# A decoder trunk on one core: where ScalarE's lead copies and two of its table loads stand in the queue

## The chip, the cores and the metric

The kernel runs on one core of one Trainium2 chip. The core's engines work beside each other, each on its own list of instructions in order, and wait for one another through semaphores: TensorE (PE in the profile, its weight loads PEld), VectorE (DVE), ScalarE (ACT), GpSimd (POOL) and SyncE (SP), which here issues most of the transfers from memory. The metric is the device time of one execution in microseconds (us). The time before is the median of three runs.

## What is computed

The reference is a decoder trunk of two layers for 512 tokens of width 1024 in float32. Every layer is a mixer between two half-step SwiGLU feed-forward networks (FFNs) of inner width 2816, each behind an RMSNorm; the mixer of the first layer is a gated linear attention (GLA), that of the second a stick-breaking attention (SB).

```python
def swiglu(h, w_gate, w_up, w_down):
    return (jax.nn.silu(h @ w_gate) * (h @ w_up)) @ w_down
...
    for i in range(DEPTH):
        x = x + 0.5 * swiglu(rmsnorm(x, ffn1_norm[i]), ffn1_w_gate[i], ffn1_w_up[i], ffn1_w_down[i])
        h = rmsnorm(x, mix_norm[i])
        ...
        x = x + y.astype(x.dtype)
        x = x + 0.5 * swiglu(rmsnorm(x, ffn2_norm[i]), ffn2_w_gate[i], ffn2_w_up[i], ffn2_w_down[i])
    return rmsnorm(x, final_norm)
```

## The kernel before

**Numbers in two parts.** Every float32 operand of a large product is split into a high part in the format fp32r, which ScalarE makes by a cast, and a low part, the difference, which VectorE makes by a subtraction. A product is then three matmuls: high by high, low by high, high by low (`mm3`, and `prod` in the blocks below).

**Weights.** `Feed` holds a queue of entries. An entry is a piece of a weight matrix with the products that use it. `Feed.start` (from line 139) takes the next entry, and for it and the entries just behind it has the raw weights loaded into tile `raw` or `rawd` by SyncE (line 91), and cut into the tiles `wh` and `wl`, of which there are four each (`Entry.split`: the cast is line 126, the subtraction line 127). So casts run ahead of the products, as far as buffers allow: a cast has to wait until PE no longer needs the `wh` that it overwrites.

**The FFN blocks.** Most of the gate and up products are made in `FFN.seven` (products in line 692): a block of 256 columns by 512 tokens is made from seven half-size products in place of eight, on sums and differences of weights (DVE, lines 675 to 682, tile `s`) and of activations. A block is two entries. `body_1` starts with the product on tile `ps_w`, which ScalarE copies to `ps_z` (line 716) before PE goes on adding to both, then one on `ps_q` (line 719), again `ps_w` (line 722) and `ps_z`. `body_2` adds a third time to `ps_w`, ScalarE copies that state to `u3` (line 734, u in the profile), PE makes the 12 matmuls of the last product on `ps_q`, and then adds to `ps_w` once more. That last product overwrites what line 734 reads, so PE has to wait until the copy is done. `gate` (line 702) applies Silu on ScalarE, or multiplies with the gate on VectorE (line 705). The down products are made in `down` (line 66, tile `ps_d`) and in `seven_down` (line 367), which is built like `seven` with its copies in lines 385 and 409.

**The lead copy.** The first matmul of a block that follows a product of another kind takes its weights not from `wh` but from a small tile of its own, `first` (128 by 128, tag `w1`, one buffer): it holds the same numbers as the first 128 columns of that entry's first `wh`, made from `raw` by a second ScalarE copy (line 132). The profile calls this copy w<-raw, 32 of them in the run.

**Activations.** `FFN.cut` (line 785) splits activations: the cast on ScalarE is line 786, the subtraction on VectorE line 787. `close`, `close_first` and `close_second` use it for the products of an FFN, `normed_input` and `sums` for its input.

**Tables.** ScalarE needs a table of functions loaded for Silu, another for Exp and Ln, another for Sqrt. Two loads are written out by hand and ordered behind the last Silu of an FFN: `exp_ln_tables(st["silu"])` (line 888, the load itself in line 580) at the start of an FFN that follows an FFN, which happens once, and the load of the Sqrt table in line 909, in the last FFN ahead of the last down product.

**What sets the order.** The program is traced in Python, and a planner then orders each engine's instructions by their dependences, by when it expects operands and buffers to be ready, and by the order of tracing. An instruction that it takes to be ready early moves ahead of others. `tc.issue_after(i)` gives what is traced inside it, on the engine of instruction `i`, a place behind `i` in that engine's order. It sets the order of issue only; it adds no wait for `i` to finish. Before the change the lead copy has no such mark: it depends on the raw weights and on the free tile `w1` alone, while the cast in line 126 also needs a free `wh`.

Of the kernel before, what the change touches and what calls it, by code (L numbers as in the profile page):

```python
# [18 lines left out]
P = 128  # L19
# [13 lines left out]
def decoder(ctx: ExitStack, tc: tile.TileContext, a: dict, out: bass.AP):  # L33
    nc = tc.nc
# [59 lines left out]
    class Entry:  # L94
# [14 lines left out]
        def split(self):  # L109
            if self.W is None:  # L110
                self.W = []
                for r, (_, _, n, m) in zip(self.view(), self.units):
                    few = n * m < 1024
                    if few:

                        h = st["few"].tile([P, n * m + NEAR], F32R, tag="vh", bufs=1, name="wh")[:, NEAR:]
                        l = st["few"].tile([P, n * m + 64 - NEAR], F32R, tag="vl", bufs=1, name="wl")[:, : n * m]
                    else:
                        h, l = (
                            wp.tile([P, n * m + 64], F32R, tag="w" + t, bufs=4, name="w" + t)[  # L120
                                :, self.place : self.place + n * m
                            ]
                            for t in "hl"
                        )
                    h, l = (t.rearrange("p (n m) -> p n m", m=m) for t in (h, l))
                    st["cut"] = nc.scalar.copy(h, r).ins  # L126
                    nc.vector.tensor_tensor(out=l, in0=r, in1=h.bitcast(F32), op=ALU.subtract)  # L127
                    self.W.append((h, l))
                    if self.lead and len(self.W) == 1:

                        first = wp.tile([P, P], F32R, tag="w1", bufs=1, name="w1")
                        nc.scalar.copy(first, r[:, 0, 0:P])
                        self.first = first

    class Feed:
# [321 lines left out]
    st = {}  # L457
# [79 lines left out]
    def sums_wide(pool):  # L537

        ss = st["ss"]
        h = sp.tile([P, T], F32R, tag="sq", name="sh")  # L540
        nc.scalar.copy(h, ss)
        l = pool.tile([P, T], F32R, tag="t", name="sl")
        nc.vector.tensor_tensor(out=l, in0=ss, in1=h.bitcast(F32), op=ALU.subtract)
        st["wide"] = ps = psum("ps_R")
        mm(ps, ones_r, h, True, False)
        mm(ps, ones_r, l, False, True)

    def rstd_wide():

        ps = st["wide"]  # L550
        v = sp.tile([P, T], F32, tag="ss", name="v")
        nc.vector.tensor_scalar(out=v, in0=ps, scalar1=1.0 / D, scalar2=EPS, op0=ALU.mult, op1=ALU.add)
        y = st["R"] = sp.tile([P, T], F32, tag="sq", name="R")
        act(y, v, AF.Ln)
        act(y, y, AF.Exp, scale=-0.5)
        nc.scalar.activation(ps, y, AF.Square)
        nc.vector.scalar_tensor_tensor(out=v, in0=ps, scalar=-0.5, in1=v, op0=ALU.mult, op1=ALU.mult)
        nc.vector.scalar_tensor_tensor(out=y, in0=v, scalar=1.5, in1=y, op0=ALU.add, op1=ALU.mult)

    def two_halves(between=None):  # L560

        feed.finish()
        g = [feed.start(), feed.start()]
        for i in range(3):
            for x in g:
                next(x, None)
            if i == 0 and between is not None:
                between()

    def new_norm():  # L570
        st["h"], st["l"] = st["nh"], st["nl"]

    def flush(deferred):
        for evac, ps in deferred:
            evac(ps)
        deferred.clear()

    def exp_ln_tables(after):
        with tc.issue_after(after):
            st["tab"] = nc.scalar.preload_act_table_set("natural_log_exp_and_others").ins  # L580
# [7 lines left out]
    class FFN:  # L588
# [194 lines left out]
            return t  # L783

        def cut(self, h, l, t):
            nc.scalar.copy(h, t)
            nc.vector.tensor_tensor(out=l, in0=t, in1=h.bitcast(F32), op=ALU.subtract)
            return h, l

# [90 lines left out]
        def run(self, between=None):  # L880
            with tc.tile_pool(name="hp", bufs=8, reuse_waits="tile") as self.hp, tc.tile_pool(
                name="tp", bufs=5, reuse_waits="tile"
            ) as self.tp:
                st["few"] = self.hp
                new_norm()
                if st["ss"] is not None:
                    if self.after_ffn:
                        exp_ln_tables(st["silu"])
                    two_halves(lambda: sums_wide(self.tp))
                    rstd_wide()  # L890
                flush(self.defer)
                def spread(todo, n):
                    for i in range(n):
                        for piece in todo[i * len(todo) // n : (i + 1) * len(todo) // n]:
                            piece()
                        feed.entries(1)

                spread(self.normed_input(), self.NORMED - 2)
                self.normed = True
                st["h"], st["l"] = zip(*self.n)  # L900
                todo = self.sums()
                spread(todo[:5], self.sums_by - self.NORMED)
                feed.entries(1, True)
                for piece in todo[5:]:
                    piece()
                feed.entries(self.count - self.sums_by - 1, True)
                if between is not None:
                    with tc.issue_after(st["silu"]):
                        nc.scalar.preload_act_table_set("sqrt_and_others")
                    feed.q[feed.pos].split()  # L910
                    between(self.tp)
                feed.entries(self.total - self.count)
# [579 lines left out]
    def begin(ip):  # L1492
# [116 lines left out]
        g, u = psum("ps_f"), psum("ps_f")  # L1609
        scale(0)()  # L1610
        cut(eg, 0)()
        square(0, 1, True), square(1, 1, False)
        scale(1)(), scale(2)()
# [15 lines left out]
        pin(nc.vector.tensor_scalar(out=v, in0=v, scalar1=1.0 / D, scalar2=EPS, op0=ALU.mult, op1=ALU.add))  # L1629
        low()  # L1630
        low = cut(eu, 0)
        st["sqrt"] = pin(nc.scalar.activation(y, v, AF.Sqrt)).ins
        keep(0), keep(1), keep(2)
# [26 lines left out]
        for i in range(NT):  # L1660
# [5 lines left out]
            )  # L1666
        scale(4)()
        cut(eg, 1)()
        scale(5)(), scale(6)(), scale(7)()
        st["R"] = sp.tile([P, T], F32, tag="sq", name="R")  # L1670
# [65 lines left out]
```

## Time and profile before

| | |
|---|---|
| median of 3 runs | 1842.72 us (1842.33 to 1846.41) |
| profiled execution, its own time | 1843.01 us |
| its span, first to last instruction | 1841.2 us |
| granted TensorE clock | 0.999 |
| busy: PE, PEld, DVE, ACT | 1821.4, 1656.5, 1531.1, 1068.6 us |
| matmuls on PE | 12476 |
| instructions on ACT | 1842 |
| lead copies, line 132 | 32, mean 294 ns |
| table loads on ACT, all lines | 11, 1283 ns each |

A row of a timeline gives the start in us from the start of the span, the duration in us, the engine, the line, the operation, what it writes <- what it reads, the shapes, and in square brackets how long the engine sat idle ahead of it and what released it. A row of the waits gives who waited, for whom, the idle time in total, how many times, and the longest. In the view of one line the numbers behind an operation are its count and its shortest, median and longest duration in ns; below stands for whom its engine was idle before it, with total us and times, and who waited for it. An arrow points to the releaser. The ends of matmuls are modelled, so that their starts tell more of PE's pace than their durations.

### The profile page before, as it was taken

The page shows a single profiled execution, that of the slowest core. Times are in us where ns is not written, and L with a number is a line of the kernel's source. Part 1 is how long each engine was busy: PE and PEld are TensorE (multiplying, and loading weights), DVE is VectorE, ACT ScalarE, POOL GpSimd, SP SyncE. Part 2 cuts the span into 40 slices and gives each one's busy share as a digit, 9 for nine tenths or more (in the row PEclk, how much of TensorE's full clock was granted, in tenths as well). Part 3 has the DMA queues.
Part 4 walks back from the last instruction along what each step waited for, and adds up shares of the span by engine and source line. Part 5 has one row for each costly group of instructions (what it writes and reads, how often), then busy time and mean ns, then how long its engine had stood idle before and what let it go on. Part 6 is the DMA issues. An engine that isn't in the chain of part 4 may idle for free.

```text
span 1841.2 us, 30773 instructions
## 1 busy us (share of the span) xinstructions
PE 1821.4 (99%) x12476; PEld 1656.5 (90%) x12476; DVE 1531.1 (83%) x2509; ACT 1068.6 (58%) x1842; POOL 8.7 (0%) x20
## 2 busy tenths in 40 slices
PE   8999999999999999999999999999999999999998
PEld 7999999889888899999889999998888788999997
DVE  8999797776777989889798988976878779898885
ACT  6556555444555566555555555645878755565554
POOL 0000000100000000000000000000000000000000
PEclk9999999999999999999999999999999999999999
DMA  5333324221223233333233232322221222333331
GB/s 161 118 122 116 103 93 135 83 69 47 69 69 115 92 101 107 120 100 115 89 106 113 91 118 92 119 87 83 69 70 58 69 92 92 115 106 113 104 104 69
DMA packets 177649, 179.20 MB, mean 97 GB/s; under 512 B 4130, under 2 KB 168020, under 8 KB 177508
## 3 DMA queue, kind: packets, MB, share of 16 engines
q1 hardware_dynamic: 176800, 176.18, 30.3%
q8 instruction: 97, 1.59, 0.4%
q0 software_dynamic: 608, 1.05, 0.2%
q14 instruction: 44, 0.36, 0.1%
q10 hardware_dynamic: 100, 0.03, 0.0%
HBM read 175.17 MB, written 2.10 MB: 96 GB/s over the span
## 4 chain that ended last, share of the span: by engine, by line
PE 80%; DVE 12%; DMA 6%; ACT 2%; issue 1%; SPq 0%; DVEq 0%; ACTq 0%
PE ps_w L692 16%; PE ps_f L66 15%; PE ps_d L66 14%; PE ps_q L692 7%; PE ps_t L66 5%; DVE wl L127 4%; PE ps_z L692 4%; PE ps_b L66 4%; PE ps_w L367 3%; DMA raw<-in_ffn_w_gate_dram 3%; DMA raw<-in_ffn_w_up_dram 3%; PE ps_q L367 2%; PE ps_S L66 1%; PE ps_z L1315 1%; PE ps_bt L66 1%
## 5 line engine op out<-in xcount | busy, mean ns | idle before, releaser
L127 DVE TENSOR_TENSOR wl<-raw,wh 128x1024 fp32r<-128x1024 f32 x242 | 255.5, 1059 | 88.9 <-ACT wh L126 46.6
L126 ACT CAST wh<-raw 128x1024 fp32r<-128x1024 f32 (+1 forms) x242 | 223.0, 922 | 163.0 <-PE ps_d L66 36.5
L127 DVE TENSOR_TENSOR wl<-s,wh 128x1024 fp32r<-128x1024 f32 x176 | 213.9, 1217 | 43.4 <-PE ps_z L692 40.1
L692 PE MATMUL ps_w<-th,wh 128*128 128x256 f32 x864 | 240.1, 278 | 5.6 <-ACT u L734 5.3
L692 PE MATMUL ps_w<-tl,wh 128*128 128x256 f32 x864 | 238.8, 276 | 0.0
L692 PE MATMUL ps_w<-th,wl 128*128 128x256 f32 x864 | 238.7, 276 | 0.0
L126 ACT CAST wh<-s 128x1024 fp32r<-128x1024 f32 x176 | 184.8, 1050 | 84.0 <-DVE s L682 27.7
L66 PE MATMUL ps_f<-xh,wh 128*128 128x512 f32 x432 | 172.6, 400 | 0.0
L66 PE MATMUL ps_f<-xl,wh 128*128 128x512 f32 x432 | 169.4, 392 | 0.0
L692 PEld LDWEIGHTS ps_w<-th,wh 128*128 128x128 f32 x864 | 162.2, 188 | 8.0 <-ACT u L734 7.0
L66 PE MATMUL ps_f<-xh,wl 128*128 128x512 f32 x432 | 168.9, 391 | 0.0
L692 PEld LDWEIGHTS ps_w<-tl,wh 128*128 128x128 f32 x864 | 162.3, 188 | 0.0
L66 PE MATMUL ps_d<-hh,wl 128*128 128x512 f32 x416 | 162.2, 390 | 0.0
L692 PEld LDWEIGHTS ps_w<-th,wl 128*128 128x128 f32 x864 | 162.2, 188 | 0.0
L66 PE MATMUL ps_d<-hh,wh 128*128 128x512 f32 x416 | 162.2, 390 | 0.0
L66 PE MATMUL ps_d<-hl,wh 128*128 128x512 f32 x416 | 161.8, 389 | 0.0
L126 ACT CAST wh<-rawd 128x1024 fp32r<-128x1024 f32 (+1 forms) x84 | 81.5, 970 | 89.9 <-PE ps_d L66 48.8
L127 DVE TENSOR_TENSOR wl<-rawd,wh 128x1024 fp32r<-128x1024 f32 (+1 forms) x84 | 93.1, 1116 | 21.1 <-PE ps_z L692 12.0
L322 DVE SCALAR_TENSOR_TENSOR x<-ps_d,x 128x512 f32<-128x512 f32 x120 | 80.7, 683 | 22.1 <-PE ps_d L66 21.7
L66 PEld LDWEIGHTS ps_f<-xl,wh 128*128 128x128 f32 x432 | 81.1, 188 | 17.3
L66 PEld LDWEIGHTS ps_f<-xh,wl 128*128 128x128 f32 x432 | 81.3, 188 | 15.6
L66 PEld LDWEIGHTS ps_f<-xh,wh 128*128 128x128 f32 x432 | 81.3, 188 | 15.4
(348 smaller groups left out, 5271.4 us busy)
## 6 DMA issues: line engine op xcount, KB each, us to landing
raw<-in_ffn_w_gate_dram SPq DMA_DIRECT2D x43, 1024.0 KB, 5.4
raw<-in_ffn_w_up_dram SPq DMA_DIRECT2D x43, 1024.0 KB, 5.6
rawd<-in_ffn_w_down_dram SPq DMA_DIRECT2D x84, 512.0 KB, 3.7
raw<-in_gla_w_in_dram SPq DMA_DIRECT2D x12, 1024.0 KB, 5.3
raw<-in_sb_w_in_dram SPq DMA_DIRECT2D x16, 512.0 KB, 3.8
raw<-in_gla_w_out_dram SPq DMA_DIRECT2D x4, 1024.0 KB, 5.0
raw<-in_sb_w_in_dram SPq DMA_DIRECT2D x4, 1024.0 KB, 5.3
raw<-in_sb_w_out_dram SPq DMA_DIRECT2D x4, 1024.0 KB, 5.0
```

The costliest lines, as they stand in the source:

```text
L66: st["pe"] = nc.tensor.matmul(ps, l, r, start=first, stop=last).ins
L126: st["cut"] = nc.scalar.copy(h, r).ins
L127: nc.vector.tensor_tensor(out=l, in0=r, in1=h.bitcast(F32), op=ALU.subtract)
L322: nc.vector.scalar_tensor_tensor(out=xs[k], in0=ps, scalar=0.5, in1=xs[k], op0=ALU.mult, op1=ALU.add)
L367: st["pe"] = nc.tensor.matmul(ps, l_, r_, start=first and c + n == 0, stop=c == 1 and n == 2, skip_group_check=True).ins
L692: st["pe"] = nc.tensor.matmul(o, l_, r_, start=first and j + n == 0, stop=j == 3 and n == 2, skip_group_check=True).ins
L1315: nc.tensor.matmul(o_, l_, r_, start=first, stop=last, skip_group_check=True)
```

## The change

Three edits, all on ScalarE's order, none on what is computed. The lead copy is marked to be issued behind `st["cut"]`, which at that point is the cast (line 126) of the same raw block. `FFN.cut` keeps its latest cast as `st["closed"]`. The two hand-written table loads are marked behind that cast in place of the last Silu.

```diff
@@ Entry.split
                     if self.lead and len(self.W) == 1:
 
                         first = wp.tile([P, P], F32R, tag="w1", bufs=1, name="w1")
-                        nc.scalar.copy(first, r[:, 0, 0:P])
+                        with tc.issue_after(st["cut"]):
+                            nc.scalar.copy(first, r[:, 0, 0:P])
                         self.first = first
@@ FFN.cut
-            nc.scalar.copy(h, t)
+            st["closed"] = nc.scalar.copy(h, t).ins
             nc.vector.tensor_tensor(out=l, in0=t, in1=h.bitcast(F32), op=ALU.subtract)
@@ FFN.run
                     if self.after_ffn:
-                        exp_ln_tables(st["silu"])
+                        exp_ln_tables(st["closed"])
@@ FFN.run
                 if between is not None:
-                    with tc.issue_after(st["silu"]):
+                    with tc.issue_after(st["closed"]):
                         nc.scalar.preload_act_table_set("sqrt_and_others")
```

## The prediction, made before the changed kernel ran

> **What bounds the kernel now.** I read the page first, then the waits of PE, then the source view of the copies that the change moves, then the timelines of ACT and PE around them.
>
> ```profile
> span 1841.2 us, 30773 instructions
> PE 1821.4 (99%) x12476; PEld 1656.5 (90%) x12476; DVE 1531.1 (83%) x2509; ACT 1068.6 (58%) x1842; POOL 8.7 (0%) x20
> PE 80%; DVE 12%; DMA 6%; ACT 2%; issue 1%; SPq 0%; DVEq 0%; ACTq 0%
> ```
>
> PE sets the time from end to end. An edit on ACT, busy for 58%, is therefore worth exactly the time in which PE stands still because of ACT. PE's own waits, longest first:
>
> ```profile
> PE ps_w L692 <- ACT u L734: 5.3, 9, 1.2
> ...
> PE ps_w L367 <- ACT ps_z L385: 1.3, 2, 0.9
> ...
> PE ps_w L692 <- ACT ps_z L716: 0.4, 2, 0.2
> ```
>
> The largest wait is nine times for the copy u of line 734; two are for the copy of line 716. Neither copy is slow; what matters is what ACT was doing just before. Line 132 is the lead copy:
>
> ```profile
> L132 ACT CAST w<-raw x32: 287/293/300, 50.6 to 1757.0; 128x128 fp32r<-128x128 f32 x32
>   DMA raw<-in_ffn_w_up_dram: 11.4, 8
>   DMA raw<-in_ffn_w_gate_dram: 4.8, 5
> ```
>
> At 13 of its 32 places ACT sits idle ahead of the lead copy, 16.2 us in all, until a weight transfer lands. ACT works in order, so whatever stands behind waits too. ACT around the first such place, and the ninth of the places where PE waits:
>
> ```profile
> 86.57 0.30 ACT L132 CAST w<-raw 128x128 fp32r<-128x128 f32 x1 [1.20 <-DMA raw<-in_ffn_w_up_dram]
> 86.78 0.36 ACT L734 COPY u<-ps_w 128x256 f32<-128x256 f32 x1
> ...
> 93.56 1.05 ACT L126 CAST wh<-raw 128x1024 fp32r<-128x1024 f32 x1
> ...
> 1649.52 0.30 ACT L132 CAST w<-raw 128x128 fp32r<-128x128 f32 x1 [1.39 <-DMA raw<-in_ffn_w_up_dram]
> 1649.72 0.37 ACT L734 COPY u<-ps_w 128x256 f32<-128x256 f32 x1
> ```
>
> The lead copy waits to 86.57, u starts 0.21 us later, and the cast that reads the same raw block comes only at 93.56. So it is in the timeline at all nine PE waits for u: the instruction ahead of u is a lead copy held by its transfer. The remaining four held copies (13 less 9) cost PE nothing.
>
> **What one such stall costs.** The idle time in brackets is not the whole loss, because ends of matmuls are modelled: a product of 256 columns is shown 0.28 us long while the next starts 0.11 us after it. So I take starts:
>
> ```profile
> 86.61 0.28 PE L692 MATMUL ps_q<-nh,wl 128*128 128x256 f32 x1
> 86.72 0.28 PE L692 MATMUL ps_q<-nl,wh 128*128 128x256 f32 x1
> 87.19 0.38 PE L692 MATMUL ps_w<-th,wh 128*128 128x256 f32 x1 [0.20 <-ACT u L734]
> 87.42 0.29 PE L692 MATMUL ps_w<-th,wl 128*128 128x256 f32 x1
> 87.54 0.28 PE L692 MATMUL ps_w<-tl,wh 128*128 128x256 f32 x1
> ```
>
> From 86.72 to 87.54 are 0.82 us for three steps that take 3 x 0.113 = 0.34 elsewhere in the same stream: 0.48 lost, where 0.20 is shown. Each stall thus costs its shown idle time plus 0.28: 0.17 hidden under the modelled end (0.28 less 0.11) and 0.11 because the first product after the wait takes two steps.
>
> [...]
>
> ```profile
>   PEld ps_w L692: 7.0, 9
> ```
>
> Among those who waited for line 734, the weight loads stand with 7.0 us in nine waits: they were held along with the matmul, so I keep the 0.11.
>
> **Part 1, the lead copies.** Nothing is added or removed: 32 copies of 0.29 us (0.21 from start to start, 86.57 to 86.78) go behind a cast of the same raw block. No wait for completion is added: only their place in ACT's order changes. No DMA goes with them. On SP the next load into raw waits for the last reader of it, and behind that cast DVE still reads the block for 1.2 us in line 127, so a lead copy 0.3 us behind the cast is never last.
>
> *Removed:* nine stalls, 5.3 + 9 x 0.28 = 7.8 us. What is late next there? Without the copy in the way u starts when its product is complete, as it does at undisturbed places (rows at 110.66 and 111.82 below): it ends at 111.03, and PE, which has 12 products of ps_q to do meanwhile, overwrites the tile at 111.82. 0.79 us remain, so PE runs through.
>
> *Added:* the copy must now be ready for PE's first product. I compare cast and first use in the first and last of 32 blocks:
>
> ```profile
> 54.10 1.05 ACT L126 CAST wh<-raw 128x1024 fp32r<-128x1024 f32 x1
> ...
> 1773.02 1.05 ACT L126 CAST wh<-raw 128x1024 fp32r<-128x1024 f32 x1 [1.88 <-PE ps_w L367]
> 1774.33 1.05 ACT L126 CAST wh<-s 128x1024 fp32r<-128x1024 f32 x1 [0.26 <-PE ps_z L367]
> ```
> ```profile
> 69.16 0.28 PE L692 MATMUL ps_w<-nh,w 128*128 128x256 f32 x1
> ```
> ```profile
> 1783.67 0.28 PE L692 MATMUL ps_w<-nh,w 128*128 128x256 f32 x1
> ```
>
> Cast end to first use is 14.0 us in the first (69.16 less 55.15) and 9.6 in the last; the 0.21 us of the copy vanish in that. Queued behind the copy are a cast of sums and then u. The commonest surroundings:
>
> ```profile
> 108.21 1.05 ACT L126 CAST wh<-raw 128x1024 fp32r<-128x1024 f32 x1
> 109.30 1.05 ACT L126 CAST wh<-s 128x1024 fp32r<-128x1024 f32 x1
> 110.66 0.37 ACT L734 COPY u<-ps_w 128x256 f32<-128x256 f32 x1 [0.31 <-PE ps_w L692]
> ```
> ```profile
> 111.82 0.28 PE L692 MATMUL ps_w<-th,wh 128*128 128x256 f32 x1
> ```
>
> ACT has 0.31 us to spare ahead of u, more than 0.21; in the last block the 0.26 us of idle time behind the cast hold it. Even if u were 0.21 late, the 0.79 us ahead of PE's next product on the tile would cover it. I cost the new place at 0; without cover it is 32 x 0.21 = 6.7 us.
>
> **Part 2, the table loads.**
>
> ```profile
> 881.39 1.28 ACT L580 ACT_TABLE_LOAD   x1
> 882.69 0.36 ACT L716 COPY ps_z<-ps_w 128x256 f32<-128x256 f32 x1
> ...
> 891.85 0.61 ACT L786 CAST hh<-o 128x512 fp32r<-128x512 f32 x1
> 896.00 1.05 ACT L126 CAST wh<-rawd 128x1024 fp32r<-128x1024 f32 x1 [3.55 <-PE ps_d L66]
> ```
> ```profile
> 1805.43 0.62 ACT L786 CAST hh<-o 128x512 fp32r<-128x512 f32 x1 [1.45 <-DVE o L705]
> 1808.91 1.06 ACT L126 CAST wh<-raw 128x1024 fp32r<-128x1024 f32 x1 [2.86 <-PE ps_d L66]
> ```
>
> Today a load of 1.28 us stands ahead of a copy of line 716; that is the last row of PE's waits, twice (the other load, line 909, stands likewise). Gain: 0.4 + 2 x 0.28 = 0.9 us. Behind the last cast of activations ACT is idle for 3.55 and 2.86 us until PE frees a buffer, and 1.28 fits both times: cost 0. Without that cover it would be 2 x 1.28 = 2.6 us at most.
>
> [...]
>
> **The sum.** 7.8 + 0.9 = 8.7 us. The profiled execution took 1843.0 us (span 1841.2 and 1.8 around it): 1834.3. It lies 0.3 above the median of 1842.7, so **1834.0**. Bounds: if only the shown idle time comes back (5.7), 1837.0. The order of instructions is planned anew from the dependences, so untouched waits can change too: if the two of line 385 went as well (1.3 + 2 x 0.28 = 1.9), 1832.1. This replanning is the one thing the trace cannot show; I take 0 for it, since ACT's total work is the same.
>
> **Rivals.**
>
> *The late transfer only moves the wait.* PE now arrives up to 1.5 us earlier at everything behind a late block. For it: 13 waits for the same transfers. Against it: the full cast of the block comes 7 us after the lead copy (86.57 against 93.56) and has over 9 us to its use. If the stalls of over half a microsecond came back by half, some 3 us return: 1837 to 1839.
>
> *The copy at its new place delays u and the products.* For it: it is now just ahead of casts that end close to u. Against: 0.31 us idle there and 0.79 behind. All 32 on the path: 1842.7 - 8.7 + 6.7 = 1840.7, no measurable change.
>
> *Nothing moves*, since the copies stay ahead of u: 1842.7, or 1841.8 with the tables alone. Against: today's copies stand 7 us ahead of their casts, so the new order forces them to move.
>
> *Slower: the freed slot goes to a cast.* If the new plan puts a full cast of the late block ahead of u, ACT waits for the same transfer and then holds u for 1.05 us in place of 0.21. Price: nine stalls stay and each grows by 0.84, 7.6 us, with the tables 6.7 net: 1849.4. It decides from two such places of 0.84 up if the nine stalls otherwise stay. Against: the cast needs a weight buffer that PE frees only later (the last block's was held 1.88 us by PE, not by DMA).
>
> **How the numbers follow.** Forecast 0.74 (1832.1 to 1837.0), moved wait 0.07, delay by the copy 0.07, nothing moves 0.02, slower 0.10. The range runs from the forecast's low end over the moved wait: 1832.0 to 1839.5. A difference under 0.2% (3.7 us) cannot be told from none: faster 0.81, same 0.09, slower 0.10.
>
> **What would show it.** Right: PE's row for u L734 gone or under 0.5 us, that for ps_z L716 gone; no idle time for DMA ahead of the lead copy; each lead copy right behind a cast of raw; the loads in the gaps before a cast that waits for ps_d; PE's busy time lower by about 3 us and the span by 8 to 9. Wrong: a new PE row for the lead copy's tile or wh L126, u still behind a wait for raw, or other ACT copies, such as that of line 385, with longer waits than today.

## The result, and the profile after

| | before | after |
|---|---|---|
| median on one chip | 1845.21 us (1842.33 to 1846.48, 6 runs) | 1837.72 us (1837.11 to 1841.85, 6 runs) |
| profiled execution, its own time | 1843.01 us | 1839.01 us |
| its span | 1841.2 us | 1837.2 us |

The ratio is 0.9966, 95% interval 0.9953 to 0.9979: faster by about a third of a per cent. Two repeats of the comparison, told below, gave 0.9973 and 0.9961. Executions of either kernel differ by several us among themselves; why, the experiments show.

The page of the changed kernel, its line of busy times:

```profile
PE 1821.0 (99%) x12476; PEld 1657.2 (90%) x12476; DVE 1530.1 (83%) x2509; ACT 1068.4 (58%) x1842; POOL 8.7 (0%) x20
```

The span is 4.0 us shorter, not 8 to 9, and PE's busy time fell by 0.4 us, not by 3. So something came back. All line numbers are two higher than before from the lead copy on. First what the change did. PE's longest waits after it, but for those on the first input:

```profile
PE ps_q L369 <- DVE o L707: 1.4, 1, 1.4
PE ps_w L369 <- ACT ps_z L387: 1.2, 2, 0.7
```

The row of nine waits for u is gone, and so is the one for the two copies that stood behind a table load. The groups show the lead copy; the last number is the idle time of ACT ahead of all 32:

```profile
L134 ACT CAST w<-raw 128x128 fp32r<-128x128 f32 x32 | 9.5, 296 | 0.0
```

ACT's 16.2 us of idle time ahead of lead copies have become 0.0. At the first place that the prediction showed (u was held to 86.78), ACT's timeline now reads:

```profile
85.83 0.37 ACT L736 COPY u<-ps_w 128x256 f32<-128x256 f32 x1 [0.36 <-PE ps_w L694]
...
93.40 1.05 ACT L126 CAST wh<-raw 128x1024 fp32r<-128x1024 f32 x1
94.35 0.30 ACT L134 CAST w<-raw 128x128 fp32r<-128x128 f32 x1
```

u waits for PE's product alone, and the lead copy starts right behind the cast of its block. PE at this place:

```profile
86.83 0.28 PE L694 MATMUL ps_q<-nl,wh 128*128 128x256 f32 x1
86.94 0.28 PE L694 MATMUL ps_w<-th,wh 128*128 128x256 f32 x1
87.05 0.28 PE L694 MATMUL ps_w<-th,wl 128*128 128x256 f32 x1
87.17 0.28 PE L694 MATMUL ps_w<-tl,wh 128*128 128x256 f32 x1
```

Three steps take 0.34 us where they took 0.82: 0.48 are saved, as the prediction worked out. PE issues the same products in the same order in both kernels, so I set the k-th start of one trace against the k-th of the other. At the eleven stalls the difference steps by 0.48, 0.57, 1.54, 0.79, 0.92, 1.07, 1.22, 0.51 and 0.67 (lead copies) and 0.47 and 0.47 (tables): **8.7 us** in all. The two table loads stand in their gaps:

```profile
892.45 1.28 ACT L582 ACT_TABLE_LOAD   x1
895.56 1.05 ACT L126 CAST wh<-rawd 128x1024 fp32r<-128x1024 f32 x1 [1.83 <-PE ps_d L66]
...
1802.10 1.28 ACT L911 ACT_TABLE_LOAD   x1
...
1804.93 1.06 ACT L126 CAST wh<-raw 128x1024 fp32r<-128x1024 f32 x1 [1.55 <-PE ps_d L66]
```

After each, 1.83 and 1.55 us of the gap are still left. Nothing else moved: ACT's order differs in 34 places (32 copies, 2 loads), and that of PE, DVE, GpSimd and SyncE in none.

**What came back.** The same alignment shows one large step the other way, 3.8 us between 853 and 862. PE, around it:

```profile
853.83 0.28 PE L369 MATMUL ps_q<-hl,wh 128*128 128x256 f32 x1
855.54 0.38 PE L369 MATMUL ps_q<-hh,wh 128*128 128x256 f32 x1 [1.43 <-DVE o L707]
...
856.23 0.28 PE L369 MATMUL ps_q<-hl,wh 128*128 128x256 f32 x1
856.65 0.39 PE L369 MATMUL ps_w<-hh,wh 128*128 128x256 f32 x1
```

PE waits for the cast of o (ACT, line 788), which waits for DVE's products of line 707. DVE at that time:

```profile
853.45 0.69 DVE L677 TENSOR_TENSOR s<-raw 128x512 f32<-128x512 f32 x1 [2.41 <-DMA raw<-in_ffn_w_up_dram]
854.06 0.42 DVE L740 TENSOR_TENSOR o<-ps_q,o 128x256 f32<-128x256 f32 x1
...
855.07 0.42 DVE L707 TENSOR_TENSOR o<-ps_w,o 128x256 f32<-128x256 f32 x1
```

This is the lead copy's pattern on another engine. Line 677, the first of the sums of a weight block, stood at the head of DVE's queue for 2.41 us until its block came, and the short work on the path stood behind it. Before the change the same instruction did not wait:

```profile
854.58 0.69 DVE L675 TENSOR_TENSOR s<-raw 128x512 f32<-128x512 f32 x1
```

It is not the block that had held the lead copy a little earlier, but the next one. Its transfer, from issue to landing (last number), first before, then after the change:

```profile
raw<-in_ffn_w_up_dram SPq DMA_DIRECT2D x1, 1024.0 KB, 6.5
```
```profile
raw<-in_ffn_w_up_dram SPq DMA_DIRECT2D x1, 1024.0 KB, 8.1
```

It was issued 2.5 us earlier (845.30 against 847.80), took 1.6 longer, and landed 0.9 us earlier, while PE had come 3.6 us earlier. The last term is a surprise. A row of the windows gives the stretch, its length, busy time and count of PE, PEld, DVE, ACT and POOL, the granted clock, the share of DMA and GB/s:

```profile
856.93:860.34 3.41, 3.41 (x18) 3.41 (x18) 2.89 (x7) 0.90 (x1) 0.00 (x0) 0.50 0.76 261
```

For 3.41 us after the stall TensorE got half its clock (0.50): 18 products where 30 fit (3.41 / 0.113), 12 x 0.113 = 1.4 us. With 1.43 + 0.17 + 0.11 = 1.7 for the stall and 0.42 - 0.11 = 0.3 for the next wait (856.23 to 856.65) that is 3.4 of the 3.8. The other 0.9 of the 4.7 that came back (8.7 - 4.0) is the sum of smaller differences of both signs.

### The profile page after: what moved, and what is told of

The parts are those of the page before. It is cut to its first block, busy times and chain, and to the rows that moved or that the text cites. A ratio compares the mean times of both kernels' runs of the same rounds, so it can differ in the third digit from the quotient of the medians.

```text
span 1837.2 us, 30777 instructions
## 1 busy us (share of the span) xinstructions
PE 1821.0 (99%) x12476; PEld 1657.2 (90%) x12476; DVE 1530.1 (83%) x2509; ACT 1068.4 (58%) x1842; POOL 8.7 (0%) x20
## 3 DMA queue, kind: packets, MB, share of 16 engines
q8 instruction: 97, 1.59, 0.4%
```

## The experiments

Theory 1: the change takes 8.7 us out, and late weight blocks give part of it back through DVE's line 677. Rival: the new order on ACT itself costs something (the copy at its new place, or casts behind it).

**The changed kernel again**, unedited, as a yardstick for the three that follow.

> The changed kernel once more, as the yardstick for the others on this chip. Theory: the nine waits for the copy u and the two behind a table load are gone for good (8.7 us by the starts of PE's products), and some 3 to 4 us come back where DVE now waits for the same late weight block in line 677 and PE then waits for the copy to ps_z (lines 718 and 387) or for ps_q (line 369); so about 5 to 6 us below the kernel before, ratio 0.997. Where PE stands still for over a microsecond its granted clock may fall to 0.5 for 3.4 us, as it did once at 857 us of the changed kernel's profile, which costs about 1.6 us in that execution alone. Rival, that nothing comes back and the 4 us of the profiles were the clock alone: ratio 0.9953.

Measured: 1837.34 us (1833.62 to 1840.20, 8 runs), ratio 0.9973 (0.9961 to 0.9984).

**The lead copies alone.**

```diff
-                        nc.scalar.copy(first, r[:, 0, 0:P])
+                        with tc.issue_after(st["cut"]):
+                            nc.scalar.copy(first, r[:, 0, 0:P])
```

> Only the lead copies are moved; the two table loads stand behind the last Silu as before. Theory: 0.9 us more than the full change (two PE waits for line 718 of 0.19 us shown idle each, 0.46 by starts, at the two loads), no PE wait for u. Rival, that the loads cost or bring something else, such as 1.3 us each: 2.6 us more than the full change, or the same time.

Measured: 1835.55 us, ratio 0.9966 (0.9954 to 0.9978), span 1833.8. The waits of PE keep the row of the tables, and the one for u is gone:

```profile
PE ps_w L694 <- ACT ps_z L718: 0.4, 2, 0.2
```

The copies carry the gain: with and without the tables the time is the same within the intervals. The 0.9 us that the expectation had on top of the full change did not show; the median is 1.8 us below that of the full change, inside the scatter of either.

**The table loads alone.**

```diff
-                        exp_ln_tables(st["silu"])
+                        exp_ln_tables(st["closed"])
...
-                    with tc.issue_after(st["silu"]):
+                    with tc.issue_after(st["closed"]):
```

> Only the two table loads are moved; the lead copies stand where they stood before. Theory: 0.9 us less than the kernel before, ratio 0.9995; all nine PE waits for u stay with 5.3 us shown idle, and DVE's wait in line 677 for up_dram stays at about 1.6 us. Rival, that the gain of the change is in the loads: ratio 0.997.

Measured: 1839.15 us (1837.91 to 1844.64, 12 runs), ratio 0.9989 (0.9981 to 0.9998). The 0.9 us that the prediction had for this part lie inside the interval (0.0002 to 0.0019 of 1841.7 us are 0.4 to 3.5 us), but the waits did not come as expected. Those of PE and DVE:

```profile
PE ps_w L693 <- ACT u L735: 2.7, 4, 1.1
```
```profile
DVE s L676 <- DMA raw<-in_ffn_w_gate_dram: 5.3, 11, 1.6
DVE s L676 <- DMA raw<-in_ffn_w_up_dram: 4.0, 5, 1.5
```

Four waits for u in place of nine, with the lead copies where they always were. Idle time that ends under a modelled end is not in that row: by its starts PE still lost 5.5 us behind held lead copies here, where it lost 7.8 in the profile of before. And DVE waits 4.0 us for the up weights, where the profile of before had 1.6 in two waits. So how late a block is differs from execution to execution, and one profile is one draw. DVE's larger wait in the profile after the change is therefore not by itself the mark of the change.

**Each lead copy twice.** If the new place cost anything, a second copy there would double it.

```diff
                             nc.scalar.copy(first, r[:, 0, 0:P])
+                            nc.scalar.copy(first, r[:, 0, 0:P])
```

> The changed kernel with each of the 32 lead copies issued twice in a row into the same tile. Theory: the place behind the cast is free, so the same time as the changed kernel within 0.1%, though ACT works 32 x 0.21 = 6.7 us more. Rival, that the copy at its new place delays u and the products and so gave back what is missing: up to 6.7 us more than the changed kernel, with PE waits for u or ps_z grown by 0.2 us per block.

Measured: 1835.06 us (1834.69 to 1839.10, 5 runs), ratio 0.9967 (0.9955 to 0.9979), no slower than the changed kernel, and ACT busy for 1074.2 us in place of 1068.4. The new place is free; this part of the rival falls.

**The changed kernel once more**, as the yardstick of the next three.

> The changed kernel as the yardstick on this chip. Theory: PE's waits for the copies to ps_z (lines 718 and 387) and for ps_q (line 369) together 1.5 to 4 us shown idle, differing from run to run with how late the weight blocks land, since DVE's line 677 waits for them; ratio 0.996 to 0.998 to the kernel before.

Measured: 1836.58 us (1834.27 to 1838.99, 5 runs), ratio 0.9961 (0.9947 to 0.9974).

**DVE's sums without the weights.** Lines 677 and 678 read the identity, so DVE never waits for a block there. The sums of the weights are left out of what is computed; number and size of instructions stay.

```diff
+            four_i = ident.unsqueeze(1).to_broadcast([P, 4, P])
...
-                nc.vector.tensor_tensor(out=s[:, 0:4], in0=t[:, 0:4, P:], in1=t[:, 4:8, P:], op=ALU.add)
-                nc.vector.tensor_tensor(out=s[:, 4:8], in0=s[:, 0:4], in1=t[:, 0:4, 0:P], op=ALU.subtract)
+                nc.vector.tensor_tensor(out=s[:, 0:4], in0=four_i, in1=four_i, op=ALU.add)
+                nc.vector.tensor_tensor(out=s[:, 4:8], in0=s[:, 0:4], in1=four_i, op=ALU.subtract)
```

> The changed kernel, where the two VectorE operations that make the first sums of a gate or up block (lines 677 and 678) read the constant identity in place of the raw weights: the sums are left out, the operations, their sizes and their place stay, but they wait for no transfer. Theory: DVE's waits for raw in line 677 disappear, and with them PE's waits for ps_q in line 369 and most of those for the copies to ps_z; PE's idle time after the first 30 us falls from 4.3 us (two profiles of the changed kernel) to under 1.5, the time by 3 to 5 us: ratio 0.994 to 0.995. Rival, that ScalarE's own order holds the copies to ps_z, behind two casts of 0.5 us (line 788): those waits stay at 1.2 us or more and the time falls by less than 1 us.

Measured: 1828.41 us (1828.15 to 1829.07, 4 runs), ratio 0.9923 (0.9909 to 0.9936): 8.2 us under the yardstick run beside it, more than I expected. The runs now differ by 0.9 us, where the yardstick's differ by 4.7. DVE at the place of the big stall:

```profile
848.15 0.69 DVE L678 TENSOR_TENSOR s<-ident 128x512 f32<-128x512 f32 x1
848.75 0.42 DVE L741 TENSOR_TENSOR o<-ps_q,o 128x256 f32<-128x256 f32 x1
```

PE's waits in lines 369 and 694 are gone altogether, those for line 387 with them, which stood in the profile of before too; what is left is the start of the program and 0.4 us. On SP the loads wait for line 127 as before (184 times in both kernels), so the edit does not let them start ahead of it. So DVE standing at late blocks is what stops PE in the changed kernel, and it is the source of the scatter. ACT's new order has no part in it.

**The same with the change undone.** The same edit on the kernel before; against the last run it has the change taken back and nothing else.

> The kernel before, with the sums of lines 675 and 676 taken from the identity in place of the gate and up weights, as e_sumfree does to the changed kernel: the products of those sums are left out of what is computed, at the same number and size of instructions. DVE then no longer stands at late weight blocks; ACT's lead copies and table loads stand where they stood before. Against e_sumfree (ratio 0.9923, 1828.4 us) it has the change undone and nothing else. Theory (the change takes out its stalls in full, some 8.7 us, and only DVE's waits for later blocks give part of it back): with DVE's waits out of both, the whole price of the stalls shows, ratio 0.9960 to 0.9985 (1835 to 1840 us), with the PE row ps_w <- u at 4 us or more. Rival (the change is worth no more than the 5 us it showed even where nothing takes anything back): ratio 0.994 to 0.9955.

Measured: 1836.55 us (1834.98 to 1840.13, 12 runs), ratio 0.9978 (0.9968 to 0.9988). The time is as the theory had it; the rival's 0.994 to 0.9955 lies outside the interval. The rows of PE and ACT:

```profile
PE ps_w L693 <- ACT u L735: 1.6, 3, 0.8
```
```profile
ACT w L132 <- DMA raw<-in_ffn_w_up_dram: 8.6, 8, 1.9
...
ACT w L132 <- DMA raw<-in_ffn_w_gate_dram: 2.4, 3, 1.1
```

The lead copies are still held at ACT's head, 11 times here. My 4 us for u missed: 1.6 are shown. By its starts PE lost 3.84 us at nine such places and 0.92 at the two loads, 4.8 together. Yet the profiled spans differ by 1834.5 - 1827.3 = 7.2 us, the medians by 8.1, and the ratios by 0.9923 / 0.9978 = 0.9945. Most of the rest of the 7.2 is PE's pace, which the prediction's price of a stall left out. The second product after the first stall and the last product ahead of the next down products, in this kernel and then in the one with the change:

```profile
87.94 0.28 PE L693 MATMUL ps_w<-th,wl 128*128 128x256 f32 x1
99.01 0.28 PE L693 MATMUL ps_w<-tl,wh 128*128 128x256 f32 x1
```
```profile
87.35 0.28 PE L695 MATMUL ps_w<-th,wl 128*128 128x256 f32 x1
98.00 0.28 PE L695 MATMUL ps_w<-tl,wh 128*128 128x256 f32 x1
```

The same 94 steps take 11.07 us behind the stall and 10.65 without it: 0.118 each in place of 0.113. Four of the eleven stalls here have such a tail, 1.7 us together; in the profile of before two have one (0.8 us behind the stall at 273, 0.4 behind that at 1571). Why only some stalls are followed by it these traces do not show; stretches of this pace also stand where no lead copy is near, the longest after the change 1.1 us from 1052 to 1082. **In this pair, where DVE takes nothing back, the change is worth some 7 to 10 us, and 4 to 7 us in the kernel as it is** (4.3 to 7.5 by the medians of the three comparisons).

Theory 2, an attempt at a better kernel: if line 677 leaves DVE's head, the rest comes too. Five kernels tried it, in three forms.

**The sums queued late**, behind the subtraction of line 127 for the same block, and laid down only there (`late` names the sums); on the changed kernel, then on the one before.

```diff
-                self.views = [view(ch.load()) for ch, view, _, _ in self.units]
+                self.views = [None if late(view) else view(ch.load()) for ch, view, _, _ in self.units]
...
+                    if r is None:
+                        with tc.issue_after(st["sub"]) if i else ExitStack():
+                            r = view(ch.load())
```

> The changed kernel, with the same step done on VectorE: the first sums of a block (lines 677 and 678) are issued behind the subtraction (line 127) of the same raw block, and so at a time when that block has long landed. All the work is done. Theory: DVE no longer waits for transfers in line 677, as with the sums left out, so ratio 0.994 to 0.995. Rival: the sums now come so late that their cast and subtraction are not ready for the block's second product; then PE waits for wl or wh of sums, and the time is that of the changed kernel or above it.

> The kernel before, with VectorE's first sums issued behind the subtraction of the same raw block and the lead copies and table loads left where they were. Theory: the late block still holds ScalarE at the lead copy, so the nine PE waits for u stay (about 5 us shown idle), while the waits for ps_z in line 387 (1.3 us) go: 1 to 2 us below the kernel before. Rival, that VectorE alone was what counted: as fast as with both, ratio 0.995.

Measured: 1858.14 us, ratio 1.0085 (1.0071 to 1.0099), and 1861.95 us, ratio 1.0105 (1.0091 to 1.0118). Both are slower. PE's longest waits in the first:

```profile
PE ps_w L700 <- ACT u L742: 6.9, 8, 0.9
PE ps_q L375 <- DVE o L713: 5.3, 6, 1.8
```

DVE no longer waits for transfers in these sums. But PE now waits for u and for o: my times for both kernels were wrong. For the first the rival's time came, above that of the changed kernel, though not by the waits for wl or wh that it named. That the casts of the late sums crowd u and o is my reading, not tested apart.

**The sums early in the program, only line 677 moved back** past the youngest subtraction of line 127; again on both kernels.

```diff
+                    st["sub"] = nc.vector.tensor_tensor(out=l, in0=r, in1=h.bitcast(F32), op=ALU.subtract).ins
...
+                with tc.issue_after(st["sub"]): nc.vector.tensor_tensor(out=s[:, 0:4], in0=t[:, 0:4, P:], in1=t[:, 4:8, P:], op=ALU.add)
```

> The changed kernel with one thing more: the first of the two sums of lines 675 to 678 (line 677) is queued on DVE behind the youngest subtraction of line 127 that is laid down by then. Unlike in e_sumlate the sums stay early in the program and so do the casts that read them; only the instruction that waits for the late weight block is moved back past work that is ready. Theory (what the late blocks gave back is what waits behind line 677 on DVE; e_sumlate lost by its late casts, not by the move itself): DVE's waits of line 677 for the gate and up transfers fall from 12 to 14 us to under 9, PE's waits ps_q <- o of lines 369 and 707 and the drop of the granted clock behind them are gone or rarer, no new groups of PE waits over 1 us, and the time lies between e_sumfree and the changed kernel: 1830 to 1835 us, ratio 0.991 to 0.995. Rival (any later place on DVE for the sums comes late for the casts that read them, as in e_sumlate): new PE waits for u of 3 us and more, ratio 1.000 to 1.006. No effect: 0.996 to 0.997.

> The kernel before with the same move of line 675 (its number there) and nothing else. The lead copies still stand at ACT's head, so by the theory a late block still stops PE at the same nine places through ACT, and taking the wait out of DVE gains little: ratio 0.998 to 1.001, with the PE waits ps_w <- u of 4 to 6 us still there. If DVE's wait was the dearer one all along and ACT's was not needed, the ratio is that of e_sumsub against the changed kernel carried over: 0.995 to 0.997. If the later place comes late for the casts: 1.003 to 1.009.

Measured: 1847.45 us, ratio 1.0031 (1.0019 to 1.0043), and 1849.11 us, ratio 1.0040 (1.0027 to 1.0054). Both theories had less; the times are those of the rivals. The waits for u that the first rival had (3 us and more) did not come, and those that were to stay in the second kernel (4 to 6 us) are 0.7 in two. Against the changed kernel, PE's starts show that the stall at 855 went (a step of 2.8 us), as did those at 745 and 1044 (1.0 each), and that eight new ones of about 1.5 us came. The first kernel's waits of PE, and DVE at one of the eight:

```profile
PE ps_q L369 <- DVE o L707: 6.4, 6, 1.3
PE ps_w L369 <- DVE x L375: 5.1, 4, 1.3
```
```profile
254.46 1.22 DVE L127 TENSOR_TENSOR wl<-raw,wh 128x1024 fp32r<-128x1024 f32 x1
...
256.20 0.69 DVE L127 TENSOR_TENSOR wl<-rawd,wh 128x512 fp32r<-128x512 f32 x1
256.80 0.69 DVE L677 TENSOR_TENSOR s<-raw 128x512 f32<-128x512 f32 x1
257.40 0.42 DVE L707 TENSOR_TENSOR o<-ps_w,o 128x256 f32<-128x256 f32 x1
```

The last product of a gate (line 707, from ps_w) stands behind two subtractions and the sum. In the changed kernel, at the same place of the work, it came behind the sum but ahead of both subtractions:

```profile
253.85 0.69 DVE L677 TENSOR_TENSOR s<-raw 128x512 f32<-128x512 f32 x1
...
255.46 0.42 DVE L707 TENSOR_TENSOR o<-ps_w,o 128x256 f32<-128x256 f32 x1
255.79 1.22 DVE L127 TENSOR_TENSOR wl<-raw,wh 128x1024 fp32r<-128x1024 f32 x1
```

One mark on one line made the planner order its surroundings anew: some 290 of DVE's 2509 instructions stand in another order than in the changed kernel, and some 25 of ACT's.

These two pairs also say what the change is worth when DVE's sums do not wait for blocks and PE comes later for other reasons: 3.8 us with the sums queued late (1861.95 - 1858.14) and 1.7 with line 677 moved back (1849.11 - 1847.45). By PE's starts, the kernels with the lead copies in their old place lose 2.9 and 1.2 us behind held lead copies, and 0.9 and 1.2 behind the table loads. So in these pairs the change is worth about the stalls that it takes out, and these slower kernels have fewer of them.

**Line 677 behind the youngest product of line 707** in place of the subtraction.

```diff
+                with tc.issue_after(st["mul"]) if "mul" in st else ExitStack(): nc.vector.tensor_tensor(out=s[:, 0:4], in0=t[:, 0:4, P:], in1=t[:, 4:8, P:], op=ALU.add)
```

> The changed kernel with the first sum (line 677) queued on DVE behind the youngest multiplication of line 707 laid down by then, in place of the youngest subtraction of line 127 as in e_sumsub. In e_sumsub the planner then put the subtraction of rawd and the sum itself ahead of the last multiplication of a gate (o<-ps_w): that came 1.9 us later than in the changed kernel, and PE stood still 1.5 us for it at the head of each seven-product down projection. Here that multiplication stands ahead of the sum again, with only one subtraction in between. Theory (the loss of e_sumsub is that crossing alone): DVE's waits of line 677 for the gate and up transfers stay below 9 us, PE's waits ps_q <- o of lines 369 and 707 fall from 6.4 us to under 3, and the time is 1832 to 1838 us, ratio 0.993 to 0.997. Rival (every move of the sum past planned work on DVE costs as much as the late block does): PE waits of 4 us and more for DVE, ratio 1.000 to 1.005.

Measured: 1858.23 us, ratio 1.0084 (1.0069 to 1.0098), above the theory and above the rival's range too. The waits for o did fall, but others came:

```profile
PE ps_q L694 <- DVE x L375: 8.6, 4, 2.1
...
PE ps_q L369 <- DVE o L707: 1.3, 2, 0.7
```

PE now waits for the sums of the residual (line 375), four times for 2.1 us, and each time a drop of the granted clock to 0.50 follows. What follows for theory 2: the price of DVE's wait is shown, some 8 us, but no place that I tried for the instruction is cheaper than the one it has. No version beat the changed kernel. A third buffer for raw blocks, which might let them come earlier, was not tried.

## Why the prediction came out as it did

The measured 1837.72 us lies in the range (1832.0 to 1839.5) and the sign was right, but it lies above the forecast's own range (1832.1 to 1837.0), in that of the rival to which I gave 0.07. That it lies so near is luck in part: the forecast took 8.7 from 1842.72, while the six runs before have a median of 1845.21; the difference is 7.5 here, and 4.3 and 5.5 in the two repeats. By the steps:

- *What bounds the kernel*: right. Only PE's standing still counted. ACT's busy time is the same.
- *Nine stalls, 7.8 us, and two, 0.9*: right in size at the places themselves, 7.8 and 0.9 by PE's starts, and idle time plus 0.28 held at the place shown in full. The price left out the slower pace that follows some of the stalls. What the trace of before could not show is that the size of the nine is one draw: in two executions of other kernels with the lead copies in their old place PE lost 5.5 and 3.8 us by its starts, of which the rows show 4 and 3 waits.
- *The new place at 0*: right; a second copy there costs nothing either.
- *The table loads at 0, hidden in their gaps*: right, 1.83 and 1.55 us stayed free.
- *Replanning at 0*: right; only the 34 moved instructions changed place. (It is not small in general: a mark on line 677 moved much else.)
- *"What is late next there?"*: this step failed. I answered it for PE's tile at the same place (0.79 us to spare) and stopped. The next thing late was the next weight block, and the engine to be held was DVE. The row for it stood in the profile, and I had not read it:

```profile
DVE s L675 <- DMA raw<-in_ffn_w_gate_dram: 7.3, 12, 1.7
DVE s L675 <- DMA raw<-in_ffn_w_up_dram: 1.6, 2, 1.4
```

  After the change, in its profile:

```profile
DVE s L677 <- DMA raw<-in_ffn_w_gate_dram: 7.5, 12, 1.9
DVE s L677 <- DMA raw<-in_ffn_w_up_dram: 5.0, 5, 2.4
```

- *Rival "the late transfer only moves the wait", 0.07*: mispriced. My argument against it spoke of the full cast of the same block on ACT, 7 us later. DVE reads each block too, and often before that cast. Its price of some 3 us was near what happened: 8.7 less the 4.3 to 7.5 us by which the three comparisons' medians differ is 1 to 4 us. That these come back through DVE is shown by the two kernels without its waits; how much of it is the new order's own doing and how much a draw of the transfers, single profiles cannot tell, the less so as the 8.7 are a draw too.
- *Slower, a cast in the freed slot*: did not happen; the cast of the block stands at its old place, 93.40 against 93.56.
- *PE's busy time lower by about 3*: it fell by 0.4. The halved clock stretched products (18 where 30 fit). In the run of the lead copies alone, without such a drop, it is 1818.4, 3.0 lower.

## What to carry to other kernels

When an instruction that waits for a late transfer is taken from the head of one in-order queue, look through every other queue for readers of the same stream of transfers, and read what stands behind them: the gain is what remains when the next of them has taken its share. A wait's size in one profile is one draw; two kernels with the suspected wait made impossible in both measure the price better than the wait row does, though only for as many stalls as that pair has. And a mark that moves one instruction in a planned order is free only if the trace shows that nothing else moved.

## What the hardware showed that I had not expected

TensorE's granted clock fell to 0.50 after PE had stood still for 1.6 to 2.3 us. In all 14 traces, counted from start to start less one step of 0.11 us, away from the first 30 us: after 21 gaps of 1.2 to 1.45 us the clock never fell; after 6 gaps of 1.5 to 1.95 us it fell once (the one of 1.6 at 855.54 above); after 5 gaps of 2.0 to 2.3 us it fell five times. Each drop lasted 3.413 us at 0.50. One of the five, from the last kernel, PE's stall and the window behind it:

```profile
721.91 0.28 PE L694 MATMUL ps_w<-nl,wh 128*128 128x256 f32 x1
724.33 0.47 PE L694 MATMUL ps_q<-th,wh 128*128 128x256 f32 x1 [2.14 <-DVE x L375]
```
```profile
724.48:727.89 3.41, 3.41 (x17) 3.41 (x18) 2.77 (x5) 0.37 (x1) 0.00 (x0) 0.50 0.69 240
```

In the kernel with each copy twice, after a gap of 1.7 us, the clock stayed whole:

```profile
855.00:858.40 3.40, 3.40 (x31) 3.39 (x31) 3.40 (x9) 1.93 (x4) 0.00 (x0) 1.00 0.75 264
```

Six of these gaps by length, and the granted clock behind each:

| kernel | gap, us | granted clock behind it |
|---|---|---|
| the changed kernel, at 855 | 1.59, and shorter ones behind it | 0.50 |
| each lead copy twice | 1.74 | 1.00 |
| sums queued late, on the one before | 1.80 | 1.00 |
| sums queued late | 1.93 | 1.00 |
| the changed kernel again | 2.05 | 0.50 |
| line 677 behind line 707, last of four | 2.30 | 0.50 |

So between 1.59 and 1.93 us the length of the gap alone does not decide here, and what does was not shown. The drop at 857 cost some 1.4 us on top of the stall (12 x 0.113, above). The kernel with each copy twice stood still at the same place of the work, for 1.74 us against 1.59, without a drop, so the one at 857 was a draw as well, as far as these two profiles tell.
